# A two-layer encoder with an RWKV-7 scan: the triangular blocks inverted from blocks of 8 instead of 16

## Chip, cores and metric

The kernel runs on one core of a Trainium2 chip. The metric is the device time of one execution in microseconds (us); the kernel before was timed in three runs. Engines are named PE (TensorE, the matmul array), DVE (VectorE), ACT (ScalarE), POOL (GpSimd) and SP (SyncE, which here only issues DMAs).

## The reference, cut to what matters

Layer 0 is differential attention and a dense SwiGLU; layer 1 is two-way RWKV-7 time mixing (16 heads of 64, 272 tokens, of which 16 are learned meta tokens) and a mixture of 8 SwiGLU experts, top 2. The part at hand is the recurrence of layer 1, once forward and once backward over the tokens:

```
def _wkv7_step(S, inp):
    r, w, k, v, kk, a = inp
    sa = einsum('bhvk,bhk->bhv', S, kk)
    S = S * w - sa * (kk * a) + v * k          # outer products
    y = einsum('bhvk,bhk->bhv', S, r)
    return S, y
_, y_fwd = lax.scan(_wkv7_step, S0, (r, decay0, kd0, v, kk, a0))
_, y_bwd = lax.scan(_wkv7_step, S0, (r, decay1, kd1, v, kk, a1), reverse=True)
```

The kernel computes it by chunks of 64 tokens. Inside a chunk the steps depend on each other through a strictly triangular 64 x 64 matrix Q for each head, direction and chunk, and (1 - Q)^-1 turns the chunk's steps into a few matrix products.

## The kernel before, in words

All is float32. Layer 0 comes first, then the projections of layer 1, then the scan, then the experts, whose weights (1 MB loads by SP) are most of the data. The scan takes the 16 heads as 8 pairs (f = 0 to 7); a pair has two heads, two directions and four chunks, so 8 blocks (q) of 64 rows for each head, the first head on partitions 0 to 63, the second on 64 to 127.

A pair goes through four steps in `rwkv`:
- `rv` (L682): receptance and values by matmuls (L701), a few after each step of an earlier pair's recurrence;
- `prep` (L747): decays, rates, factors and the pairwise products, of which the masked blocks QC (L825, L833) are the Q above; `meta` (L846) makes the 16 x 16 block of the meta tokens, which goes to QD as a ninth block (L858, L859);
- `solve` (L1152): `inverse`, then `values`;
- `chain` (L965): the recurrence over the chunks, with high priority, and `norm`.
While `chain` of pair f runs, `solve` of f + 1 and `prep` of f + 2 are under way.

`inverse` (L892) works so:
- the four 16 x 16 diagonal blocks of each Q are picked out: POOL multiplies QC by a mask (L898, tile inv_p) and DVE sums over the blocks (L900, tile QD). POOL also masks QC for the first doubling level into QL (L904, one instruction for each head) and sets TD to unit matrices (L906);
- 15 rounds on DVE (L907 to L911), each a shuffle, a product and a sum that need each other in turn, solve the rows of all 9 blocks at once; round i works on 9 x (16 - i) columns, so 9 in the first and 135 in the last;
- POOL spreads TD back into 64 x 64 blocks (L913, tile T) and makes the meta tokens' Tm (L916);
- the level from 16 to 32: DVE transposes (L921), 16 matmuls with QL (L925, bank pi), ACT copies to RT (L928), 16 matmuls with RT (L932), DVE adds (L934). In the profile a float32 matmul is two records;
- the level from 32 to 64 (L937 to L963), whose result is TF, in a tile named w_raw; L963 is its last copy. `chain` begins with L990 and needs TF and Tm.

Tiles of the inverse have one buffer (QL, RT, TD, T16) or two (QC, QD, inv_b, inv_s); PSUM bank pi has one, pa two. There is one instruction stream for each engine, in order. Which order it is, the framework's planner works out ahead of the run from its own estimate of durations; the order of the calls, priorities (`CHAIN_PRIORITY`) and `issue_after` guide it. So an edit in one step can shift others within the scan.

Of the kernel before, what the change touches and what calls it, by code (L numbers as in the profile page):

```python
# [8 lines left out]
F32 = mybir.dt.float32  # L9
# [3 lines left out]
OP = mybir.AluOpType  # L13
AX = mybir.AxisListType
PSUM = bass.MemoryType.PSUM

D = 1024
NF = 8
T = 272
# [14 lines left out]
# tables that depend on the shapes alone: name -> (table, first column, columns)  # L34
LAYOUT, WIDTH = {}, [0, 0, 0, 0]
for _t, _n, _w in ((0, 'ident', 128), (1, 'ones_h', 128), (1, 'ones_d', 128), (1, 'toep', 448),
                   (2, 'bones', 128), (2, 'gmask', 384), (2, 'blk16', 64), (2, 'lev', 64), (2, 'eye16', 16),
                   (2, 'seg', 277), (2, 'sel', 128), (3, 'slot', 128), (3, 'before', 128), (3, 'one', 128), (3, 'tie', 64)):
    LAYOUT[_n] = (_t, WIDTH[_t], _w)
    WIDTH[_t] += _w  # L40


def const_tables():
    import numpy as np
    p, r = np.arange(128)[:, None], np.arange(128)[None, :]
# [10 lines left out]
    c['blk16'] = rb == cb  # L56
    c['lev'] = (rb // 2 == cb // 2) & (cb > rb)
    c['eye16'] = (p % 16) == np.arange(16)[None, :]
# [16 lines left out]
# the order of the steps that prepare a head pair's scan: of the first one, of the others  # L75
# [4 lines left out]
CHAIN_PRIORITY = 100     # how many instructions ahead of the rest of the scan the recurrence is issued  # L80


class Trunk:
# [4 lines left out]
    # ---------------------------------------------------------------- helpers  # L88
# [10 lines left out]
    def load(self, src, r0, kt, c0, nc_, pitch):  # L99
        """a [kt*128, nc_] block of a weight, as [128, kt, nc_]"""  # L100
# [4 lines left out]
    def parts(self, raw):  # L105
        """the two float32r parts of a block of up to 1024 columns"""
# [22 lines left out]
    # ---------------------------------------------------------------- LN over features on partitions  # L129
# [22 lines left out]
    def ln_end(self, pool, psum, g, b, xo, hi=None, lo=None, done=None):  # L152
        """xo(f): where the float32 result goes; hi/lo: [128, NF, T] float32r or None; done(f) follows each feature tile"""
# [42 lines left out]
    # ---------------------------------------------------------------- constants  # L196
# [31 lines left out]
    def param_rows(self, tmp):  # L228
        """per-feature parameters as they come"""
# [16 lines left out]
    def params(self, psum, tag):  # L246
        """features to the partitions"""
# [28 lines left out]
    # ---------------------------------------------------------------- layer 0  # L276
# [181 lines left out]
    def layer0(self, stack):  # L458
        """all but its last LayerNorm"""
# [66 lines left out]
        with tc.tile_pool(name="ffn", bufs=1) as fp:  # L526
# [111 lines left out]
        # first halves of the low-rank maps  # L638
# [43 lines left out]
    def rv(self, sp, psum, f, S, after=None):  # L682
        """receptance and values of head pair f, a few products after each of the given instructions"""
# [20 lines left out]
    def gates(self, sp, psum):  # L704
        """the output gate: gT holds its mixed input first"""
# [20 lines left out]
    def scan_consts(self, sp):  # L726
# [8 lines left out]
        self.QL = self.ip.tile([128, 8, 2, 64], F32, name="QL", bufs=1)  # L735
        self.RT = self.ip.tile([128, 8, 2, 64], F32, name="RT", bufs=1)
# [10 lines left out]
    def prep(self, sp, psum, f, S):  # L747
        """the factors of head pair f and their pairwise products"""
# [10 lines left out]
        QC = S['QC'] = self.ip.tile([128, 8, 64], F32, name="QC")  # L759
        QD = S['QD'] = self.ip.tile([128, 9, 16], F32, name="QD")  # L760
# [52 lines left out]
        def pairs(d):  # L813
            """pairwise products, masked: rows beta | kappa (second head kappa | beta), columns alpha | rho (rho | alpha)"""
# [3 lines left out]
            if d == 1:  # L818
                # transposed, to make it upper triangular too
# [17 lines left out]
        def turns(d):  # L837
            """beta | kappa, token-major"""
# [7 lines left out]
        def meta():  # L846
# [11 lines left out]
            nc.gpsimd.tensor_copy(QD[LO, 8, :], gsm[LO, 0, :])  # L858
            nc.gpsimd.tensor_copy(QD[HI, 8, :], gsm[HI, 1, :])  # L859
# [15 lines left out]
    def values(self, sp, psum, f, S):  # L875
        """values, token-major: chunk rows of the second head on top, of the first below"""
# [15 lines left out]
    def inverse(self, sp, psum, S):  # L892
        """(1 - Q)^-1 of the strictly upper triangular 64 x 64 blocks; those of the backward scan come out transposed"""
        nc = self.nc
        QC, QD = S['QC'], S['QD']
        b16 = self.c['blk16'].rearrange("p (b i) -> p b i", b=4)
        pr = self.ip.tile([128, 512], F32, name="inv_p", bufs=1).rearrange("p (q b i) -> p q b i", q=8, b=4)
        nc.gpsimd.tensor_tensor(pr, QC.rearrange("p q (b i) -> p q b i", b=4), b16.unsqueeze(1).to_broadcast([128, 8, 4, 16]),  # L898
                                op=OP.mult)
        nc.vector.tensor_reduce(QD[:, 0:8, :], pr.rearrange("p q b i -> p q i b"), axis=AX.X, op=OP.add)  # L900
        H = ((0, slice(0, 64)), (1, slice(64, 128)))
        QL, RT, TF = self.QL, self.RT, S['TF']
        for h, s in H:
            nc.gpsimd.tensor_tensor(QL[s, :, h, :], QC[s], self.c['lev'][s].unsqueeze(1).to_broadcast([64, 8, 64]), op=OP.mult)  # L904
        TD = self.ip.tile([128, 9, 16], F32, name="TD", bufs=1)
        nc.gpsimd.tensor_copy(TD, self.c['eye16'].unsqueeze(1).to_broadcast([128, 9, 16]))  # L906
        for i in range(15, 0, -1):  # L907
            b = self.ip.tile([128, 9, 16], F32, name="inv_b")[:, :, :16 - i]
            nc.vector.stream_shuffle(b, TD[:, :, i:16], [i] * 16 + [16 + i] * 16)
            nc.vector.tensor_tensor(b, b, QD[:, :, i:i + 1].to_broadcast([128, 9, 16 - i]), op=OP.mult)  # L910
            nc.vector.tensor_tensor(TD[:, :, i:16], TD[:, :, i:16], b, op=OP.add)  # L911
        T16 = self.ip.tile([128, 8, 64], F32, name="T16", bufs=1)
        nc.gpsimd.tensor_tensor(T16.rearrange("p q (b i) -> p q b i", b=4), TD[:, 0:8, :].unsqueeze(2).to_broadcast([128, 8, 4, 16]),  # L913
                                b16.unsqueeze(1).to_broadcast([128, 8, 4, 16]), op=OP.mult)
        Tm = S['Tm'] = sp.tile([128, 64], F32, name="Tm")
        nc.gpsimd.tensor_tensor(Tm.rearrange("p (b i) -> p b i", b=4), TD[:, 8, :].unsqueeze(1).to_broadcast([128, 4, 16]), b16,  # L916
                                op=OP.mult)
        # 16 -> 32, within masked 64 x 64 blocks
        flat = lambda t: t.rearrange("p q j -> p (q j)")
        TT = self.ip.tile([128, 512], F32, name="inv_s").rearrange("p (q j) -> p q j", q=8)  # L920
# [6 lines left out]
        for h, s in H:  # L927
            nc.scalar.copy(RT[s, :, h, :], ps[s])  # L928
# [620 lines left out]
```

## Time and profile before

| | |
|---|---|
| three runs | 1957.04, 1957.85 (median), 1960.76 us |
| profiled execution: span of its instructions | 1959.4 us; no other time is given for it |
| busy over the span | PE 1841.7 us (94%), DVE 1512.3 (77%), ACT 1186.8 (61%), POOL 632.3 (32%) |
| where the scan lies | `prep` of the first pair from about 483 us, `inverse` of the first pair from 500, last `norm` to 886 |
| experts | from about 900 us to the end |

Busy time of PE is modelled at its matmuls' ends and matmuls overlap, so a busy PE is not PE at its peak. PEclk is the clock that PE was granted as a share of 2.4 GHz; 0.5 is 1.2 GHz. "Idle before" is idle time of the engine just before an instruction, and the name after "<-" is what ended it. All times inside the trace count from the start of the span.

### The profile page before, as it was taken

The page shows a single profiled execution, that of the slowest core. Times are in us where ns is not written, and L with a number is a line of the kernel's source. Part 1 is how long each engine was busy: PE and PEld are TensorE (multiplying, and loading weights), DVE is VectorE, ACT ScalarE, POOL GpSimd, SP SyncE. Part 2 cuts the span into 40 slices and gives each one's busy share as a digit, 9 for nine tenths or more (in the row PEclk, how much of TensorE's full clock was granted, in tenths as well). Part 3 has the DMA queues.
Part 4 walks back from the last instruction along what each step waited for, and adds up shares of the span by engine and source line. Part 5 has one row for each costly group of instructions (what it writes and reads, how often), then busy time and mean ns, then how long its engine had stood idle before and what let it go on. Part 6 is the DMA issues. An engine that isn't in the chain of part 4 may idle for free. (4 is left out here: it accounts for less than half of the span.)

```text
span 1959.4 us, 30165 instructions
## 1 busy us (share of the span) xinstructions
PE 1841.7 (94%) x11332; PEld 1513.4 (77%) x11332; DVE 1512.3 (77%) x2328; ACT 1186.8 (61%) x1850; POOL 632.3 (32%) x538
## 2 busy tenths in 40 slices
PE   6999899987989989997999999999999999999996
PEld 5888899975666667776877887878878878788784
DVE  5786655587877977736888888888888888888886
ACT  4565444464254434435777777777777777777773
POOL 4322200156544634302233223232232332322323
PEclk9999899988888977898999999999999999999998
DMA  6322455521201001537899999999999999999960
GB/s 185 121 87 65 135 180 186 171 83 55 76 6 46 23 23 44 195 108 263 301 335 352 328 360 339 335 356 326 354 342 340 356 331 343 353 323 368 358 238 24
DMA packets 223997, 431.73 MB, mean 220 GB/s; under 512 B 12425, under 2 KB 77410, under 8 KB 223842
## 3 DMA queue, kind: packets, MB, share of 16 engines
q1 hardware_dynamic: 220914, 427.78, 62.5%
q10 hardware_dynamic: 2800, 1.81, 0.3%
q8 instruction: 91, 1.49, 0.3%
q0 software_dynamic: 128, 0.13, 0.1%
q14 instruction: 64, 0.52, 0.1%
HBM read 428.64 MB, written 1.05 MB: 219 GB/s over the span
## 5 line engine op out<-in xcount | busy, mean ns | idle before, releaser
L115 DVE TENSOR_TENSOR w_lo<-w_raw,w_hi 128x1024 fp32r<-128x1024 f32 (+1 forms) x632 | 884.2, 1432 | 190.4 <-ACT w_hi L112 187.1
L112 ACT CAST w_hi<-w_raw 128x1024 fp32r<-128x1024 f32 x776 | 807.0, 1049 | 332.6 <-PE pgu L124 138.4
L115 POOL TENSOR_TENSOR w_lo<-w_raw,w_hi 128x1024 fp32r<-128x1024 f32 x144 | 358.7, 2491 | 771.3 <-ACT w_hi L112 692.2
L123 PE MATMUL pgu<-w_lo,xe 128*128 128x512 f32 x896 | 356.2, 397 | 15.0 <-DVE w_lo L115 14.7
L124 PE MATMUL pgu<-w_hi,xe 128*128 128x512 f32 x896 | 353.9, 395 | 0.0
L122 PE MATMUL pgu<-w_hi,xe 128*128 128x512 f32 x896 | 349.0, 396 | 0.0
L123 PEld LDWEIGHTS pgu<-w_lo,xe 128*128 128x128 f32 x896 | 168.5, 188 | 58.1 <-DVE w_lo L115 19.0
L122 PEld LDWEIGHTS pgu<-w_hi,xe 128*128 128x128 f32 x896 | 168.4, 188 | 39.5
L124 PEld LDWEIGHTS pgu<-w_hi,xe 128*128 128x128 f32 x896 | 168.5, 188 | 39.0
L123 PE MATMUL pd<-w_lo,hth 128*128 128x512 f32 x440 | 178.1, 405 | 0.0
L124 PE MATMUL pd<-w_hi,htl 128*128 128x512 f32 x440 | 173.2, 396 | 2.3 <-DVE htl L127 2.3
L122 PE MATMUL pd<-w_hi,hth 128*128 128x512 f32 x440 | 142.1, 395 | 0.0
L124 PEld LDWEIGHTS pd<-w_hi,htl 128*128 128x128 f32 x440 | 82.2, 188 | 22.1 <-DVE htl L127 5.3
L122 PEld LDWEIGHTS pd<-w_hi,hth 128*128 128x128 f32 x440 | 82.5, 187 | 20.1
L123 PEld LDWEIGHTS pd<-w_lo,hth 128*128 128x128 f32 x440 | 82.7, 188 | 17.4
L122 PE MATMUL pj<-xh,w_hi 128*128 128x272 f32 x192 | 61.0, 318 | 8.7 <-ACT w_hi L112 5.1
L124 PE MATMUL pj<-xh,w_lo 128*128 128x272 f32 x192 | 59.1, 308 | 0.4 <-DVE w_lo L115 0.4
L123 PE MATMUL pj<-xl,w_hi 128*128 128x272 f32 x192 | 59.1, 308 | 0.0
L1330 DVE TENSOR_TENSOR hid<-hid,pgu 128x512 f32<-128x512 f32 x56 | 38.4, 686 | 20.1 <-PE pgu L124 20.0
L141 POOL COPY ln_s<-ln_y 128x272 f32<-128x272 f32 x2 | 0.8, 412 | 156.5 <-DVE ln_y L138 156.5
L701 PE MATMUL pf<-xs_v,w_raw 128*128 128x272 f32 x128 | 49.5, 518 | 0.0
L122 PEld LDWEIGHTS pj<-xh,w_hi 128*128 128x128 f32 x192 | 39.9, 208 | 10.1 <-ACT w_hi L112 5.5
(603 smaller groups left out, 3506.1 us busy)
## 6 DMA issues: line engine op xcount, KB each, us to landing
w_raw<-in_moe_w_gate_dram SPq DMA_DIRECT2D x111, 1024.0 KB, 6.7
w_raw<-in_moe_w_up_dram SPq DMA_DIRECT2D x111, 1024.0 KB, 7.3
w_raw<-in_moe_w_down_dram SPq DMA_DIRECT2D x111, 1024.0 KB, 7.0
w_raw<-in_attn_w_in_dram SPq DMA_DIRECT2D x12, 1024.0 KB, 12.2
w_raw<-in_rw_w_rkv_dram SPq DMA_DIRECT2D x12, 1024.0 KB, 5.0
w_raw<-in_ffn_w_gate_dram SPq DMA_DIRECT2D x11, 1024.0 KB, 7.9
w_raw<-in_ffn_w_up_dram SPq DMA_DIRECT2D x11, 1024.0 KB
w_raw<-in_ffn_w_down_dram SPq DMA_DIRECT2D x8, 1024.0 KB, 5.0
```

What stands on the lines that cost most here:

```text
L112: nc.scalar.copy(hi, raw)
L115: self.parted = eng.tensor_tensor(lo, raw, hi.bitcast(F32), op=OP.subtract)
L122: mm(ps, wh, xh, start=start, stop=False)
L123: mm(ps, wh, xl, start=False, stop=False)
L124: return mm(ps, wl, xh, start=False, stop=stop)
L141: nc.gpsimd.tensor_copy(self.ln_s[:, 0, :], y)
L701: nc.tensor.matmul(ps, w[:, k, o:o + 128], x[:, k, :], start=k == 0, stop=k == NF - 1)
L1330: nc.vector.tensor_tensor(s, s, ph[1], op=OP.mult)
```

## The change

The rounds stop at blocks of 8: 7 rounds instead of 15, on 9 x (8 - i) columns. A doubling level from 8 to 16 by matmuls is added in front of the level from 16 to 32; since the meta tokens' 16 x 16 block needs it too, it is now the ninth 64 x 64 block of QC (`meta` copies it there instead of to QD), and tiles of `inverse` have 9 blocks (576 columns) instead of 8 (512). QL is written twice, first with the mask of the new level, then with the old one after the first product has read it. The masked blocks pr use the two buffers of inv_s instead of inv_p. The second constants table is 56 columns wider. The rest of the diff takes comments away. Its core:

```diff
-        QC = S['QC'] = self.ip.tile([128, 8, 64], F32, name="QC")
-        QD = S['QD'] = self.ip.tile([128, 9, 16], F32, name="QD")
+        QC = S['QC'] = self.ip.tile([128, 9, 64], F32, name="QC")
+        nc.gpsimd.memset(QC[:, 8, 16:64], 0.0)
...
-            nc.gpsimd.tensor_copy(QD[LO, 8, :], gsm[LO, 0, :])
-            nc.gpsimd.tensor_copy(QD[HI, 8, :], gsm[HI, 1, :])
+            nc.gpsimd.tensor_copy(QC[LO, 8, 0:16], gsm[LO, 0, :])
+            nc.gpsimd.tensor_copy(QC[HI, 8, 0:16], gsm[HI, 1, :])
...
+        wide = lambda name, **kw: self.ip.tile([128, 576], F32, name=name, **kw).rearrange("p (q j) -> p q j", q=9)
+        pr = wide("inv_s")
+        nc.gpsimd.tensor_tensor(by8(pr), by8(QC), b8, op=OP.mult)
+        QD = self.ip.tile([128, 9, 8], F32, name="QD")
+        nc.vector.tensor_reduce(QD, by8(pr).rearrange("p q b i -> p q i b"), axis=AX.X, op=OP.add)
...
-        for i in range(15, 0, -1):
+        for h, s in H:
+            nc.gpsimd.tensor_tensor(QL[s, :, h, :], QC[s], self.c['lev8'][s].unsqueeze(1).to_broadcast([64, 9, 64]), op=OP.mult)
+        for i in range(7, 0, -1):
...
+        T8 = wide("T16", bufs=1)
+        nc.gpsimd.tensor_tensor(by8(T8), TD.unsqueeze(2).to_broadcast([128, 9, 8, 8]), b8, op=OP.mult)
+        TT = wide("inv_s")
+        nc.vector.transpose(flat(TT), flat(T8))
+        def product(left, right):
+            ps, pm = self.bank(psum).rearrange("p (q j) -> p q j", q=8), self.bank(psum, "pa")[:, 0:64]
+            for q in range(9):
+                for h, s in H:
+                    nc.tensor.matmul(ps[s, q, :] if q < 8 else pm[s], left[:, q, h, :], right[:, q, :], start=True, stop=True)
+            return ps, pm
+        ps, pm = product(QL, TT)
+        for h, s in H:
+            nc.gpsimd.tensor_tensor(QL[s, 0:8, h, :], QC[s, 0:8], self.c['lev'][s].unsqueeze(1).to_broadcast([64, 8, 64]), op=OP.mult)
+        for h, s in H:
+            nc.scalar.copy(RT[s, 0:8, h, :], ps[s])
+            nc.scalar.copy(RT[s, 8, h, :], pm[s])
+        ps, pm = product(RT, T8)
+        nc.vector.tensor_tensor(T8[:, 0:8, :], T8[:, 0:8, :], ps, op=OP.add)
         Tm = S['Tm'] = sp.tile([128, 64], F32, name="Tm")
-        nc.gpsimd.tensor_tensor(Tm ..., TD[:, 8, :] ..., b16, op=OP.mult)
+        nc.vector.tensor_tensor(Tm, T8[:, 8, :], pm, op=OP.add)
+        T16 = T8[:, 0:8, :]
```

After these lines the level from 16 to 32 goes on as before (transpose, product with QL, copy to RT, product with RT, sum).

## Rows read from the trace of the kernel before

**Rows 1.** Busy time by engine in stretches of the span: the whole scan, then four of its stretches of 10 us. Columns: stretch, length, busy time (and instructions) of PE, PE's weight loads, DVE, ACT and POOL, granted clock of PE, busy share of the DMA engines, GB/s.

```profile
495.00:895.00 400.00, 374.17 (x3643) 277.00 (x3641) 285.35 (x990) 161.30 (x502) 153.65 (x251) 0.85 0.20 71
555.00:565.00 10.00, 7.31 (x81) 6.66 (x83) 8.00 (x19) 3.03 (x8) 8.55 (x15) 0.57 0.01 2
715.00:725.00 10.00, 5.79 (x87) 4.20 (x86) 9.48 (x25) 5.13 (x14) 8.68 (x12) 0.78 0.01 2
725.00:735.00 10.00, 10.00 (x113) 6.88 (x113) 6.32 (x28) 4.68 (x16) 0.00 (x0) 0.50 0.01 3
735.00:745.00 10.00, 10.00 (x56) 6.99 (x55) 4.88 (x19) 1.79 (x6) 3.27 (x7) 0.53 0.00 1
```

**Rows 2.** The view of waits of PE, and then of DVE, in the scan (495 to 895 us): who waited for whom, us in total, times, the longest.

```profile
PE pc L1033 <- DVE R L1028: 4.7, 2, 3.3
PE pc L991 <- DVE rm L888: 4.3, 1, 4.3
PE py L1035 <- DVE R L1028: 2.5, 4, 1.3
PE py L1011 <- DVE R L986: 2.2, 5, 0.7
...
DVE R L1028 <- ACT R L1027: 17.5, 22, 2.7
DVE R L986 <- PE pc L1033: 9.9, 12, 2.2
```

**Rows 3.** The timeline of the inverse of pair 4 and of pair 7: start and length in us, engine, line, what it is. In turn: the diagonal blocks picked out, (for pair 4 only) the masking of QC by which the next pair's inverse begins, the spreading of TD after the last round, the transpose and the sum of the level from 16 to 32, and the first matmul of that pair's recurrence.

```profile
660.39 1.00 DVE L900 TENSOR_REDUCE QD<-inv_p 128x128 f32<-128x512 f32 x1
695.88 1.27 POOL L898 TENSOR_TENSOR inv_p<-QC,blob 128x512 f32<-128x512 f32 x1 [1.60 <-DVE QC L825]
705.98 1.26 POOL L913 TENSOR_TENSOR T<-TD,blob 128x512 f32<-128x512 f32 x1 [2.20 <-DVE TD L911]
708.02 0.70 DVE L921 STREAM_TRANSPOSE inv_s<-T 128x512 f32<-128x512 f32 x1
723.03 0.69 DVE L934 TENSOR_TENSOR T<-T,pi 128x512 f32<-128x512 f32 x1
741.79 0.47 PE L990 MATMUL pc<-rm,xm 64*64 64x64 f32 x2
...
800.20 1.01 DVE L900 TENSOR_REDUCE QD<-inv_p 128x128 f32<-128x512 f32 x1
824.21 1.27 POOL L913 TENSOR_TENSOR T<-TD,blob 128x512 f32<-128x512 f32 x1 [20.22 <-DVE TD L911]
825.86 0.71 DVE L921 STREAM_TRANSPOSE inv_s<-T 128x512 f32<-128x512 f32 x1
833.58 0.69 DVE L934 TENSOR_TENSOR T<-T,pi 128x512 f32<-128x512 f32 x1 [3.13 <-PE pi L932]
848.14 0.32 PE L990 MATMUL pc<-rm,xm 64*64 64x64 f32 x2
```

**Rows 4.** Groups of DVE's instructions by line and shape: the three instructions of a round, at 72 and at 135 columns (the narrowest and the widest of the eight rounds that go). Columns: times, busy us of the group, mean ns of one, idle time before.

```profile
L909 DVE STREAM_SHUFFLE inv_b<-TD 128x72 f32<-128x72 f32 x8 | 1.8, 230 | 0.1
L910 DVE TENSOR_TENSOR inv_b<-inv_b,QD 128x72 f32<-128x72 f32 x8 | 2.0, 256 | 0.3
L911 DVE TENSOR_TENSOR TD<-TD,inv_b 128x72 f32<-128x72 f32 x8 | 2.4, 304 | 0.2
L909 DVE STREAM_SHUFFLE inv_b<-TD 128x135 f32<-128x135 f32 x8 | 2.5, 314 | 0.1
L910 DVE TENSOR_TENSOR inv_b<-inv_b,QD 128x135 f32<-128x135 f32 x8 | 2.4, 304 | 0.1
L911 DVE TENSOR_TENSOR TD<-TD,inv_b 128x135 f32<-128x135 f32 x8 | 2.9, 365 | 0.1
```

**Rows 5.** The same view for DVE's other instructions of the kind that the change adds or widens: reduce, transpose, sum out of PSUM, and a 64-column operation out of PSUM.

```profile
L900 DVE TENSOR_REDUCE QD<-inv_p 128x128 f32<-128x512 f32 x8 | 8.1, 1016 | 0.0
L921 DVE STREAM_TRANSPOSE inv_s<-T 128x512 f32<-128x512 f32 x8 | 5.6, 703 | 0.6 <-POOL T L913 0.5
L934 DVE TENSOR_TENSOR T<-T,pi 128x512 f32<-128x512 f32 x8 | 5.5, 682 | 3.2 <-PE pi L932 3.1
L997 DVE COPY rm<-pc 64x64 f32<-64x64 f32 x8 | 1.8, 227 | 1.8 <-ACT rm L996 1.6
```

**Rows 6.** The timeline of PE: the first product of the level from 16 to 32 of pair 4, at full clock, and of pair 5 (the 30 records of it that follow each other), mostly at half clock.

```profile
714.95 1.15 PE L925 MATMUL pi<-inv_s,QL 128*64 128x64 f32 x32
...
759.09 1.90 PE L925 MATMUL pi<-inv_s,QL 128*64 128x64 f32 x30
```

**Rows 7.** The view by source line: instructions of ACT and POOL in the inverse, ns of one as least, median and most, first and last start, shapes.

```profile
L928 ACT COPY RT<-pi x16: 562/580/581, 534.4 to 828.6; 64x512 f32<-64x512 f32 x16
...
L898 POOL TENSOR_TENSOR inv_p<-QC,blob x8: 1266/1272/1442, 500.6 to 798.5; 128x512 f32<-128x512 f32 x8
...
L904 POOL TENSOR_TENSOR QL<-QC,blob x16: 1256/1275/1504, 501.9 to 801.2; 64x512 f32<-64x512 f32 x16
...
L916 POOL TENSOR_TENSOR Tm<-TD,blob x8: 313/322/499, 528.1 to 825.4; 128x64 f32<-128x64 f32 x8
...
L889 POOL MEMSET R<- x8: 142/145/146, 458.8 to 825.7; 64x64 f32 x8
```

**Rows 8.** The timeline of DVE and of POOL around 717 us: the same DVE instruction twice, the second beside POOL's two masks for QL.

```profile
717.23 0.42 DVE L801 SCALAR_TENSOR_TENSOR BK<-ta__7941,ep 64x256 f32<-64x256 f32 x1
717.79 1.28 DVE L801 SCALAR_TENSOR_TENSOR BK<-ta__7941,ep 64x256 f32<-64x256 f32 x1
...
717.29 2.92 POOL L904 TENSOR_TENSOR QL<-QC,blob 64x512 f32<-64x512 f32 x2
```

**Rows 9.** Busy time by engine in a stretch of the experts (columns as in rows 1), and SP's waits over the span: a weight load that waited for a product of an inverse.

```profile
1100.00:1300.00 200.00, 198.01 (x894) 160.38 (x894) 172.39 (x144) 152.16 (x164) 59.44 (x24) 1.00 0.98 346
...
SPq L102 <- PE pi L959: 23.3, 1, 23.3
```

More of the change, by code (lines that the diff above doesn't have):

```diff
@@ L36 @@
 for _t, _n, _w in ((0, 'ident', 128), (1, 'ones_h', 128), (1, 'ones_d', 128), (1, 'toep', 448),
-                   (2, 'bones', 128), (2, 'gmask', 384), (2, 'blk16', 64), (2, 'lev', 64), (2, 'eye16', 16),
+                   (2, 'bones', 128), (2, 'gmask', 384), (2, 'blk8', 64), (2, 'lev8', 64), (2, 'lev', 64), (2, 'eye8', 8),
                    (2, 'seg', 277), (2, 'sel', 128), (3, 'slot', 128), (3, 'before', 128), (3, 'one', 128), (3, 'tie', 64)):
@@ L55, in const_tables @@
     rb, cb = j // 16, r64 // 16
-    c['blk16'] = rb == cb
+    c['blk8'] = (j // 8) == (r64 // 8)
+    c['lev8'] = (rb == cb) & (r64 // 8 > j // 8)
     c['lev'] = (rb // 2 == cb // 2) & (cb > rb)
-    c['eye16'] = (p % 16) == np.arange(16)[None, :]
+    c['eye8'] = (p % 8) == np.arange(8)[None, :]
     seg = np.ones(277)
@@ L734, in scan_consts @@
         self.X = [self.kp[i // 2].tile([128, 4, 192], F32, name=f"X{i % 2}", bufs=1) for i in range(6)]
-        self.QL = self.ip.tile([128, 8, 2, 64], F32, name="QL", bufs=1)
-        self.RT = self.ip.tile([128, 8, 2, 64], F32, name="RT", bufs=1)
+        self.QL = self.ip.tile([128, 9, 2, 64], F32, name="QL", bufs=1)
+        self.RT = self.ip.tile([128, 9, 2, 64], F32, name="RT", bufs=1)
         tf = self.wraw.tile([128, 2048], F32, name="w_raw").rearrange("p (i q h j) -> p i q h j", i=2, q=8, h=2)
@@ L894, in inverse @@
         nc = self.nc
[L895 to L900, printed above, removed]
+        QC = S['QC']
@@ new lines, in inverse @@
+        wide = lambda name, **kw: self.ip.tile([128, 576], F32, name=name, **kw).rearrange("p (q j) -> p q j", q=9)
+        flat = lambda t: t.rearrange("p q j -> p (q j)")
+        by8 = lambda t: t.rearrange("p q (b i) -> p q b i", b=8)
+        b8 = self.c['blk8'].rearrange("p (b i) -> p b i", b=8).unsqueeze(1).to_broadcast([128, 9, 8, 8])
+        pr = wide("inv_s")
+        nc.gpsimd.tensor_tensor(by8(pr), by8(QC), b8, op=OP.mult)
+        QD = self.ip.tile([128, 9, 8], F32, name="QD")
+        nc.vector.tensor_reduce(QD, by8(pr).rearrange("p q b i -> p q i b"), axis=AX.X, op=OP.add)
@@ L901, in inverse @@
         H = ((0, slice(0, 64)), (1, slice(64, 128)))
         QL, RT, TF = self.QL, self.RT, S['TF']
+        TD = self.ip.tile([128, 9, 8], F32, name="TD", bufs=1)
+        nc.gpsimd.tensor_copy(TD, self.c['eye8'].unsqueeze(1).to_broadcast([128, 9, 8]))
         for h, s in H:
-            nc.gpsimd.tensor_tensor(QL[s, :, h, :], QC[s], self.c['lev'][s].unsqueeze(1).to_broadcast([64, 8, 64]), op=OP.mult)
-        TD = self.ip.tile([128, 9, 16], F32, name="TD", bufs=1)
-        nc.gpsimd.tensor_copy(TD, self.c['eye16'].unsqueeze(1).to_broadcast([128, 9, 16]))
@@ L907, in inverse @@
-        for i in range(15, 0, -1):
[L908 to L914, printed above, removed]
+            nc.gpsimd.tensor_tensor(QL[s, :, h, :], QC[s], self.c['lev8'][s].unsqueeze(1).to_broadcast([64, 9, 64]), op=OP.mult)
@@ new lines, in inverse @@
+        for i in range(7, 0, -1):
+            b = self.ip.tile([128, 9, 8], F32, name="inv_b")[:, :, :8 - i]
+            nc.vector.stream_shuffle(b, TD[:, :, i:8], [8 * k + i for k in range(4) for _ in range(8)])
+            nc.vector.tensor_tensor(b, b, QD[:, :, i:i + 1].to_broadcast([128, 9, 8 - i]), op=OP.mult)
+            nc.vector.tensor_tensor(TD[:, :, i:8], TD[:, :, i:8], b, op=OP.add)
+        T8 = wide("T16", bufs=1)
+        nc.gpsimd.tensor_tensor(by8(T8), TD.unsqueeze(2).to_broadcast([128, 9, 8, 8]), b8, op=OP.mult)
@@ L920, in inverse @@
-        TT = self.ip.tile([128, 512], F32, name="inv_s").rearrange("p (q j) -> p q j", q=8)
+        nc.vector.tensor_tensor(Tm, T8[:, 8, :], pm, op=OP.add)
+        T16 = T8[:, 0:8, :]
+        TT = wide("inv_s")[:, 0:8, :]
         nc.vector.transpose(flat(TT), flat(T16))
@@ L927, in inverse @@
         for h, s in H:
-            nc.scalar.copy(RT[s, :, h, :], ps[s])
+            nc.scalar.copy(RT[s, 0:8, h, :], ps[s])
         ps = self.bank(psum).rearrange("p (q j) -> p q j", q=8)
@@ L934, in inverse @@
         nc.vector.tensor_tensor(T16, T16, ps, op=OP.add)
-        TB = self.ip.tile([128, 512], F32, name="inv_s").rearrange("p (q j) -> p q j", q=8)
+        TB = wide("inv_s")[:, 0:8, :]
         nc.vector.transpose(flat(TB), flat(T16))
```

3 lines of the change are left out of this document (removed).

## The prediction, made before the changed kernel was run

> **What bounds the kernel now.** I read the busy time by stretches first. In the experts PE is busy 198.0 of 200 us at full clock with the DMA engines at 0.98 [rows 9]: nothing there answers to the change, and the experts' weight loads wait for tiles of the scan (SP's queue stood 23.3 us behind a product of an inverse), so a shift of the scan's end passes on one for one. The change touches only the scan, about 400 us. There PE is busy 374.2 us, idle 25.8, at a mean clock of 0.85; DVE is busy 285.4, ACT 161.3, POOL 153.7 [rows 1]. So PE bounds the scan, and two things beside its work can shrink: its idle time, and its time at half clock. A mean of 0.85 between levels of 1 and 0.5 is 30% of the scan, 120 us, at half clock. The stretches show what it follows: from 715 PE is busy 5.79 of 10 us, and in the next two stretches it is fully busy at 0.50 and 0.53 [rows 1].
>
> The waits tell who makes PE idle: four groups of PE's waits for DVE come to 4.7 + 4.3 + 2.5 + 2.2 = 13.7 us, and DVE itself waits 27.4 us in two groups for ACT and PE [rows 2]. This is a ring of the recurrence (PE, ACT, DVE, PE), whose DVE members stand in DVE's queue between rounds of a later pair's inverse. So the rounds cost PE time although no single round is what PE waits for.
>
> Last the timeline: the inverse of pair 4 takes 45.6 us from QD to T (660.39 to 705.98) and 15.7 from the level's transpose to its sum; that of pair 7 takes 23.8 (to 824.21 from the reduce's start at 800.20, call it 24.0) and 8.4 [rows 3].
>
> **What goes.** Eight of 15 rounds, those of 72 to 135 columns, three DVE instructions each. The mean of the two end widths is (230 + 314)/2 = 272 ns for the shuffle, 280 for the product, 335 for the sum [rows 4], so 0.887 us a round; 8 rounds x 8 pairs x 0.887 = 56.7 us of DVE. The seven rounds left work on the same 9 to 63 columns as the first seven before: nothing. POOL's Tm (0.32 us, [rows 7]) goes from POOL to DVE.
>
> **What comes, for each pair.** DVE: the reduce reads 576 instead of 512 columns, 1.016 x 9/8, +0.13; a transpose 0.703 x 9/8 = 0.79; a sum 0.68; Tm out of PSUM 0.23 as the nearest 64-column row [rows 5]. Together 1.83, so 14.6 for eight pairs, and DVE gets 42 us less in all.
>
> PE: two products of 18 matmuls, 72 records. 32 records took 1.15 us at full clock, 30 took 1.90 at half [rows 6]; 36 are 1.29 or 2.28, so 16 products are 20.7 to 36.5 us. At the scan's 0.85 I take 20.7/0.85 = 24. Nothing hides that: PE is the engine that is busy.
>
> ACT: two copies of 0.58 and two of 64 columns at 0.23 (taken from DVE's row, [rows 5]), 1.6, 13 in all; ACT is idle 239 us of the scan, so nothing but its place in the new level's chain. POOL: QL's first write has 9 blocks, 2 x 0.16 more; its second is 2 x 1.275 = 2.55; pr and T8 0.16 more each; the memset 0.15; Tm -0.32 [rows 7]: +3.0, 24 in all. POOL is idle 246 us of the scan, which hides it at the mean; where POOL is fully taken it costs up to these 3.0 a pair. The constants' 56 columns come with a table in layer 0 and the copies to QC replace those to QD: nothing.
>
> **New waits.** (1) QL's second write waits for PE's first product; behind it in POOL's queue stand the next pair's u, kd and BK, for which `prep` on DVE and PE waits. Bounds 0 and 2.55 a pair; I take 0, since the copy to RT, the second product, a sum and a transpose (0.58 + 1.29 + 0.68 + 0.70 = 3.3) lie before QL is read again. (2) PE's second product waits for ACT's copies; behind it stand products of the recurrence. Bounds: 0 where the planner sets other products between, 0.58 + 0.23 on two halves = 1.6 a pair; I take 0, as PE has other work nearly everywhere. (3) pr shares inv_s and so waits until the pair before has had its transpose read by L925. For pair 5 pr ran at 695.88, while L925 of pair 4 started at 714.95 [rows 3, 6]: 19 us of head start are gone as the trace stands. But the shorter rounds bring that L925 forward (below), some 12 us for pair 4, which leaves about 7, and the head start had no use while TD (one buffer) was still pair 4's until 705.98. I take 0, bound 7 on a pair like that. (4) The memset of QC waits for a buffer whose last reader, the product at L942 for two pairs before, is past by then: 0. (5) The second product's ninth block takes one of the two banks pa, which `prep` uses: 0, bound one product, 1.3. The planner lays the order anew; for that I allow 10 us either way, what one stretch of 20 us at half clock, like that from 725 to 745 [rows 1], costs or gives back.
>
> **Length of an inverse.** Eight of 15 rounds, 24 of 45 instructions: if the rest keeps its pace, the stretch from QD to T loses 45.6 x 24/45 = 24.3 us for pair 4 and 12.8 for pair 7, 18.6 in the mean. The level adds 8.4 to 15.7, mean 12, as the level from 16 to 32 takes [rows 3]. Net 6.5 shorter; the ends are 7.1 (the rounds' own time, 8 x 0.887) less 12, so 5 longer, and 18.6 less 8, so 11 shorter. The pairs overlap (chain of f beside inverse of f + 1), so this does not add up over pairs; it acts through PE's idle time and clock.
>
> **The sum.** DVE's queue loses more than half of the rounds, the wider ones. Of the 13.7 us that PE waits for DVE I let 10 go; the bounds are 0 and all 25.8 idle. The half-clock time follows idle stretches, so I let it shrink as they do, by 10/25.8, somewhat over a third: 40 us less at half clock, whose work then takes 20 at full: -20 (bounds 0 and -35). PE's new products +24. Sum -6: the profiled execution's span of 1959.4, the only time shown for it, becomes 1953.4. It lies 1.55 above the median of 1957.85, so the forecast for the median is 1952.
>
> **Rivals.** A is the forecast. **B, PE is simply the bound:** DVE's freed 42 us become idle time of DVE, the clock stays, and the 24 us on PE remain less the 10: +14, 1972. It decides as soon as PE gets back less than 24. For it: PE is busy 94% in the scan and 10.00 of 10 us from 725 to 745; the level is one more PE-ACT-PE ring for each pair. Against it: 120 us at half clock that hang on short idle stretches.
>
> **C, the level only fills PE's gaps:** the 72 records go where PE now waits (25.8 idle against 24 of new work), the recurrence keeps its times, the sum is 0: 1958. For it: totals nearly equal; against: the gaps lie in the recurrence's ring, not where the level is ready.
>
> **D, POOL's new work slows DVE:** L801 took 0.42 us by itself and 1.28 beside POOL's mask of QL, three times as long [rows 8]. In 3.0 us more of POOL a pair DVE would lose two thirds, 2.0, 16 of the 42 freed; A's 30 us of recovery shrink to 30 x 26/42 = 18.6 and the sum is +5.4: 1963. Against it: the reduce, the transpose and the ACT-bound operations need not meet the masks. The Trainium skill (SBUF — State Buffer, Who interferes with whom) says that a VectorE instruction with two SBUF inputs contends with a GpSimd instruction that reads SBUF; L801, with two such inputs, agrees by its 0.42 and 1.28. By that rule the shuffles and the transpose, with one input, would be spared, and a round's product and sum would not.
>
> **How the numbers follow.** The median can be told from no change by about 0.2%, 3.9 us. Chances: A 0.46, B 0.27, C 0.16, D 0.11. A beside the others because DVE is what the named waits end on and the clock is worth more than the idle time; B next because the new PE work is certain and its return is not. Faster: 0.41 of A, 0.02 of C, 0.01 of D = 0.44. Same: 0.05 of A, 0.02 of B, 0.12 of C, 0.04 of D = 0.23. Slower: 0.25 of B, 0.02 of C, 0.06 of D = 0.33. A's own range is 1931 (idle -16, clock -31, products at full clock +20.7: -26) to 1962. B's is 1962 to 1982 (14 and the planner's 10 each way). The range of 1931 to 1976 leaves 0.08 of A below and 0.10 of B above.
>
> **What would show it.** Right: 56 shuffles instead of 120 and DVE near 243 us in the scan; PE's matmul records up by 576; clock in the scan above 0.87; PE's waits for DVE's R and rm near 4 us; each L990 earlier than before from pair 3 on, and the last `norm` near 880 instead of 886. B shows as L990 no earlier, clock 0.85, a scan some 14 us longer with DVE idle. C: scan end unchanged, PE idle near 2. D: DVE's ns for each two-input instruction up. New waits show as PE behind RT, POOL behind the bank pi, or DVE behind inv_s. Wrong altogether if time outside 483 to 900 us changes, or if the new level takes over 20 us a pair.

## The result, and the profile after

The changed kernel took 1985.66 us (median of 4 runs, 1971.74 to 1988.24) against 1959.12 for the kernel before (4 runs): ratio 1.0123, 95% interval 1.0102 to 1.0145. It is 1.2% slower, where 1952 was forecast. The profiled execution has a span of 1984.4 us, 25.0 more than before. (The ratio is not the quotient of the two medians, which is 1.0135: one of the four runs is far shorter than the others. The two measures can differ by some tenths of a per cent.)

First the engines' totals, from the page of the changed kernel:

```profile
span 1984.4 us, 31125 instructions
PE 1864.0 (94%) x11908; PEld 1530.4 (77%) x11908; DVE 1470.6 (74%) x2096; ACT 1200.4 (60%) x1882; POOL 661.9 (33%) x554
```

Against the busy times of before (PE 1841.7, DVE 1512.3, ACT 1186.8, POOL 632.3) that is PE +22.3, DVE -41.7, ACT +13.6, POOL +29.6; the forecast had +24, -42, +13, +24. The groups that answer to [rows 5] and [rows 7] agree too (times, busy us, mean ns, idle before):

```profile
L922 DVE STREAM_TRANSPOSE inv_s<-T 128x576 f32<-128x576 f32 x8 | 6.2, 775 | 4.7 <-POOL T L919 4.6
L938 DVE TENSOR_TENSOR T<-T,pi 128x512 f32<-128x512 f32 x8 | 5.5, 688 | 12.7 <-PE pi L928 12.6
L940 DVE TENSOR_TENSOR Tm<-T,pa 128x64 f32<-128x64 f32 x8 | 1.7, 214 | 0.0
L912 POOL TENSOR_TENSOR QL<-QC,blob 64x576 f32<-64x576 f32 x16 | 22.4, 1402 | 0.6
L933 POOL TENSOR_TENSOR QL<-QC,blob 64x512 f32<-64x512 f32 x16 | 20.3, 1270 | 27.1 <-PE pi L928 22.2 <-PE pa L928 4.3
```

So the work is what it was thought to be; where it lies is not. The busy time of the scan, as in [rows 1], and of 550 to 850 us, the part in which all kernels below are in mid-scan; the second fence is the kernel before in that part:

```profile
495.00:895.00 400.00, 373.42 (x4038) 276.85 (x4037) 227.85 (x721) 167.17 (x514) 171.52 (x261) 0.85 0.17 58
550.00:850.00 300.00, 278.08 (x3169) 206.41 (x3168) 181.71 (x578) 134.55 (x418) 141.59 (x216) 0.84 0.16 55
```

```profile
550.00:850.00 300.00, 279.33 (x2906) 206.81 (x2905) 221.69 (x766) 129.07 (x409) 123.89 (x206) 0.82 0.19 65
```

DVE is relieved, but PE's idle time (26.6 of 400 us against 25.8) and its clock (0.85) are where they were. The waits of PE and of DVE in the scan (495 to 910 us), beside [rows 2]:

```profile
PE pi L969 <- DVE inv_s L960: 4.1, 2, 3.9
PE py L1034 <- DVE R L1009: 3.1, 4, 0.9
PE pa L832 <- POOL BK L804: 2.7, 2, 1.5
PE pc L1056 <- DVE R L1051: 2.5, 3, 1.3
DVE R L1051 <- ACT R L1050: 39.4, 23, 5.7
DVE R L1009 <- PE pc L1056: 18.2, 13, 2.8
```

PE's waits for DVE's R and rm did shrink, from 16.2 us (the four groups of [rows 2] and three smaller ones) to 10.0. But others came in their place, of the inverse (inv_s) and of the preparation (BK), so PE's idle time as a whole stayed. And DVE, with less to do, waits longer for the recurrence: 57.6 us in these two groups against 27.4. Now the inverses of pairs 4 and 7, beside [rows 3] (start, length in us):

```profile
650.78 0.49 ACT L769 ACTIVATE th<-pa,ptile 128x272 f32<-128x272 f32 x1 [0.93 <-PE pa L767]
678.19 0.43 DVE L827 TENSOR_TENSOR QC<-pa,blob 128x256 f32<-128x256 f32 x1 [0.19 <-PE pa L825]
681.81 1.18 DVE L905 TENSOR_REDUCE QD<-inv_s 128x72 f32<-128x576 f32 x1
693.42 1.41 POOL L919 TENSOR_TENSOR T<-TD,blob 128x576 f32<-128x576 f32 x1 [1.82 <-DVE TD L917]
695.15 0.78 DVE L922 STREAM_TRANSPOSE inv_s<-T 128x576 f32<-128x576 f32 x1
696.97 0.29 PE L928 MATMUL pa<-inv_s,QL 128*64 128x64 f32 x4
699.44 0.32 PE L928 MATMUL pa<-T,RT 128*64 128x64 f32 x4
699.67 0.69 DVE L938 TENSOR_TENSOR T<-T,pi 128x512 f32<-128x512 f32 x1 [0.90 <-PE pi L928]
699.68 0.73 PE L767 MATMUL pa<-tw,w2a 128*128 128x272 f32 x2
700.77 0.49 ACT L769 ACTIVATE th<-pa,ptile 128x272 f32<-128x272 f32 x1
729.55 0.47 PE L1013 MATMUL pc<-rm,xm 64*64 64x64 f32 x2
...
831.26 1.19 DVE L905 TENSOR_REDUCE QD<-inv_s 128x72 f32<-128x576 f32 x1
842.32 1.41 POOL L919 TENSOR_TENSOR T<-TD,blob 128x576 f32<-128x576 f32 x1 [3.69 <-DVE TD L917]
877.33 0.33 PE L1013 MATMUL pc<-rm,xm 64*64 64x64 f32 x2 [0.93 <-DVE rm L890]
```

Pair 4's stretch from QD to T is 11.6 us instead of 45.6, and its new level takes 5.2 (695.15 to the sum's end at 700.36). Yet its inverse begins 21 us later than before (681.81 against 660.39), pair 7's 31 us later. The reason is in the middle of the fence. L767 is the first matmul of the next pair's preparation; it takes a bank pa, and it follows right behind the last L928 into pa (699.44, then 699.68). So it does in every pair: the next pair's th (L769) starts at 513.5, 559.0, 601.0, 650.8, 700.8, 756.5 and 803.8 us, the sum of the new level (L938) ends at 513.4, 558.8, 600.9, 650.8, 700.4, 756.1 and 803.5. Before, nothing tied them: pair 5's th started at 669.1, 55 us ahead of pair 4's sum L934 [rows 3]:

```profile
669.14 0.49 ACT L767 ACTIVATE th<-pa,ptile 128x272 f32<-128x272 f32 x1 [0.54 <-PE pa L765]
```

Banks of one name are handed out in the order in which the program asks, and `solve` of f + 1 is written ahead of `prep` of f + 2. So preparation and inverse have become one ring: th to QC 27.4 us (650.8 to 678.2), to QD 3.6, to T 11.6, to the new sum 7.0, together 49.6 for pair 4.

The length of the scan can be taken apart into three: the first pair's first recurrence matmul (L990, L1013), the mean interval from one pair's to the next over seven intervals, and the last pair's from there to the end of its `norm`. Before: 552.6 + 7 x 42.2 + 37.8. After: 546.3 + 7 x 47.3 + 33.5. That is -6.3, +35.5, -4.3, in all +24.9 of the span's +25.0.

The mean hides where the time went. The first four intervals come to 183.3 us against 189.1 before, the last three to 147.8 against 106.3. At pair 4 the changed kernel is 12 us ahead (729.55 against 741.79), at pair 7 it is 29 behind (877.33 against 848.14). Before, the last preparations had started 33 to 57 us ahead of the previous pair's sum L934, and the last recurrences followed each other fast (39.1, 29.5 and 37.7 us apart); in the ring there is no such lead, and they stand 51.5, 49.7 and 46.6 apart.

The table gives head, interval, tail and the clock from 550 to 850 us for all runs. These four are of one profiled execution of each kernel, which can lie some us from the median of its runs (x1's 9 above, x11's 9 below, y3's 5 below, those of y4, z1 and z2 5 to 7 above). A ratio is to runs of the kernel before that were taken beside it:

```
run (edit)                          median   ratio [95%]               head   interval  tail  clock
before                              1959.1                             552.6  42.2      37.8  0.82
after                               1985.7   1.0123 [1.0102, 1.0145]   546.3  47.3      33.5  0.84
x1  after, ninth block in py        1966.9   1.0040 [1.0014, 1.0066]   545.3  45.4      37.7  0.89
x2  before, two uses of pa          2016.0   1.0275 [1.0241, 1.0309]   548.4  51.9      31.2  0.78
x3  before, level's products twice  1991.3   1.0153 [1.0128, 1.0178]   554.8  45.5      41.9  0.82
x4  before, 7 rounds                1932.6   0.9870 [0.9851, 0.9889]   527.0  41.7      37.9  0.89
x5  after, no ninth block           1957.1   1.0006 [0.9983, 1.0028]   537.6  44.1      32.4  0.93
x6  after, ninth block in pf        1968.0   1.0052 [1.0035, 1.0070]   555.7  42.8      37.8  0.88
x7  x6, pr in a buffer of its own   1979.3   1.0134 [1.0094, 1.0173]   553.5  44.8      37.9  0.88
x8  before, matmuls added to rv     1964.9   1.0045 [1.0030, 1.0059]   558.5  41.7      37.8  0.87
x9  before, 7 rounds in pair 0      1963.1   1.0039 [1.0017, 1.0061]   529.3  45.0      41.9  0.85
x10 before, 7 rounds in the others  1961.2   1.0024 [1.0001, 1.0047]   552.4  42.0      37.8  0.82
x11 new inverse in pair 0 alone     1973.6   1.0088 [1.0063, 1.0113]   540.9  44.3      37.8  0.86
x12 before, priority 80             1964.7   1.0029 [1.0003, 1.0056]   550.9  43.2      36.4  0.81
y1  after, meta block at the end    1966.9   1.0047 [1.0029, 1.0066]   550.5  44.1      34.9  0.90
y2  before, one product twice       1989.1   1.0133 [1.0101, 1.0166]   550.5  46.0      41.9  0.77
y3  after, priority 120             1953.9   0.9967 [0.9951, 0.9982]   539.8  42.8      32.4  0.92
y4  x5, priority 120                1962.7   1.0000 [0.9974, 1.0027]   541.6  45.4      34.6  0.88
z1  before, priority 120            1957.6   0.9994 [0.9976, 1.0012]   553.1  43.1      34.6  0.82
z2  after, priority 140             1956.9   0.9990 [0.9970, 1.0011]   547.0  43.1      36.0  0.93
```

### The profile page after: what moved, and what is told of

Read it like the earlier page. It is cut to its first block, busy times and chain, and to the rows that moved or that the text cites. A ratio compares the mean times of both kernels' runs of the same rounds, so it can differ in the third digit from the quotient of the medians.

```text
span 1984.4 us, 31125 instructions
## 1 busy us (share of the span) xinstructions
PE 1864.0 (94%) x11908; PEld 1530.4 (77%) x11908; DVE 1470.6 (74%) x2096; ACT 1200.4 (60%) x1882; POOL 661.9 (33%) x554
## 5 line engine op out<-in xcount | busy, mean ns | idle before, releaser
L124 PE MATMUL pgu<-w_lo,xe 128*128 128x512 f32 x896 | 356.0, 397 | 13.9 <-DVE w_lo L116 13.6
L832 PE MATMUL pa<-X,BK 128*128 128x128 f32 x256 | 46.0, 342 | 2.8 <-POOL BK L804 2.7
L832 PEld LDWEIGHTS pa<-X,BK 128*128 128x128 f32 x256 | 41.5, 246 | 6.8 <-POOL BK L804 3.8
```

What stands on the lines that cost most here:

```text
L124: mm(ps, wh, xl, start=False, stop=False)
L832: S['paired'] = nc.tensor.matmul(pg[:, c, :], BK[:, c, h, :], X[:, c, 64 * h:64 * h + 128], start=True, stop=True)
```

## The experiments

**Is it the bank?** x1:

```diff
-            ps, pm = ..., self.bank(psum, "pa")[:, 0:64]
+            ps, pm = ..., next(pms)     # the unused half of the pair's bank py
```

> The changed kernel, but the ninth blocks of the two new products go to the unused half of the bank py of the pair's own parity instead of to the banks pa. Theory R (ring): in the changed kernel the first matmul of the preparation of pair f + 2 takes the bank pa that the ninth block of pair f + 1 leaves, so preparation and inverse alternate with a fixed period of about 49 us per pair; without it the preparation runs ahead again, the last chain ends near 880 us instead of 904 and the time falls from 1985 to 1950 to 1962. Rival B (PE's 24 us of new products are the bound): the time stays within 5 us of the changed kernel's, 1980 to 1990. Rival P (the masked blocks pr wait in inv_s): also no change.

It took 1966.9, 7 above before, 19 below after; th starts 6 to 17 us ahead of the new sum again. The expectation of 1950 to 1962 was missed by 5: in pair 2 the ninth matmuls waited until 613.1 us for the `norm` of pair 0 to have read py, so this place has a wait of its own.

x2, the same dependence put into the kernel before, with hardly any work:

```diff
+        pms = [self.bank(psum, "pa")[:, 0:64] for _ in range(2)]
+        sc = self.ip.tile([128, 64], F32, name="sc")
+        for pm in pms:
+            for h, s in H:
+                nc.tensor.matmul(pm[s], QL[:, 0, h, :], TT[:, 0, :], start=True, stop=True)
+            nc.scalar.copy(sc, pm)
```

> The kernel before, with two small products (two matmuls of 64 x 64 each) into the banks pa set behind the first product of the level from 16 to 32 in each inverse, and a copy of each by ACT; nothing reads the copies. 32 matmul records and 16 copies more in all, some 5 us of engine time. Theory R: the preparation of pair f + 2 again has to wait for the inverse of pair f + 1, and the time rises by 15 to 40 us, to 1975 to 2000. Rival B: not over 5 us more, 1958 to 1964.

It took 57 us more, beyond the range expected (its 32 matmuls are 64 records, not 32). Its timeline where pair 2's inverse meets pair 3's preparation:

```profile
634.60 0.40 PE L931 MATMUL pa<-inv_s,QL 128*64 128x64 f32 x8
636.02 0.46 ACT L932 COPY sc<-pa 128x64 f32<-128x64 f32 x2
637.17 0.72 PE L765 MATMUL pa<-tw,w2a 128*128 128x272 f32 x2
638.00 0.49 ACT L767 ACTIVATE th<-pa,ptile 128x272 f32<-128x272 f32 x1 [1.52 <-PE pa L765]
```

L765, the preparation's first matmul, starts 0.7 us after the second copy has read its bank (636.48, then 637.17), and th at 638.0 instead of 584.4 in the kernel before. The interval is 51.9 us, and recurrences that used to overlap (pair 1's began 26 us before pair 0's was done) now stand 14 us or more apart. With 15 rounds in the ring it is longer than the changed kernel's. It was run at this one priority, so what part of the 57 us hangs on the order is open.

x5 leaves out the ninth block's products, and so every use of pa (Tm's upper right block is left out with them):

> The changed kernel without the ninth block's part of the two new products: 8 of 72 records a pair go, and with them every use of the banks pa by the inverse; Tm is a copy of its 8 x 8 blocks (its upper right block is left out). Theory R (the bank pa): the preparation runs ahead again and the time falls from 1985 to 1950 to 1965, at or a little below that of the kernel with the ninth block in py (1967), whose ninth block waited for the norm of two pairs before. Theory B alone (PE's new work is the bound): 1980 to 1984, as 8 records are 0.3 us a pair.

1.0006, as expected: the loss is gone, but there is no gain. Its timeline has pair 4's th 25 us ahead of pair 3's new sum:

```profile
624.82 0.49 ACT L769 ACTIVATE th<-pa,ptile 128x272 f32<-128x272 f32 x1 [0.39 <-PE pa L767]
...
649.73 0.69 DVE L937 TENSOR_TENSOR T<-T,pi 128x512 f32<-128x512 f32 x1 [2.39 <-PE pi L928]
```

x6 (`pm` from bank pf) and y1 (the ninth block through pi, behind the level from 32 to 64; inv_b gets one buffer) keep the whole computation without pa:

> The changed kernel with the ninth blocks in bank pf, which the receptance and value matmuls use, instead of in pa. Theory R: preparation does not wait; the receptance and value matmuls, which are wanted late, wait instead. 1950 to 1967. If any shared bank costs what pa costs, 1980 to 1990.

> The changed kernel, with the ninth block's part of the two new products done at the end of the inverse through the bank pi (8 records a pair, two copies and a sum moved there), so that the inverse does not use pa at all. Nothing is left out. If the bank pa is what costs 25 us, 1950 to 1966, as in the run without the ninth block (1957); if the ninth block's work itself costs, 1970 or more.

1968.0 and 1966.9: some 18 us of the 26 come back, a little past the upper end of both expectations. Each has a new cost of its own: in x6 the interval is near that of before (42.8), but the head is 9 us longer than the changed kernel's; in y1 POOL's first mask into QL waits 22.7 us in five times for the ninth block, now at the end of the inverse, to have read QL. x7 gave pr its own buffer beside x6 (`pr = wide("inv_p", bufs=1)`), and to make room three other tiles (QD, inv_b, gn_s) one buffer instead of two:

> As the kernel with the ninth blocks in pf, and the masked blocks pr have a buffer of their own again (three other small tiles get one buffer instead of two to make room). If pr's wait for the pair before costs time, 5 to 15 us below the kernel with pf alone; by the forecast, which took 0 for this wait, the same within 4 us.

11 us slower than x6 instead of faster or equal, and 22 slower than the kernel before, without the ring. Its trace shows one wait that x6 has hardly: POOL stands 29.6 us in four times, once 19.2, in front of the memset of a later pair's QC, until PE's L969 has read the old one (x6: 2.8 us in two). Whether that is the price is not shown, since buffers and order changed together. So x7 does not price pr's wait; it made the order a suspect.

**Is it PE's new work?** x3 and y2 issue the level's products of the kernel before twice (`for q in [*range(8)] * 2`), both of them or the first alone; x8 adds three matmuls of 272 columns a pair to `rv`, a similar PE time, but away from the inverse:

```diff
+                    for j in range(0 if k else 1 + i):
+                        nc.tensor.matmul(ps, w[:, k, o:o + 128], x[:, k, :], start=True, stop=True)
```

> The kernel before, with the two products of the level from 16 to 32 issued twice each into the same bank: 64 matmul records more for each pair, some 2.3 us of PE for a pair at full clock, 21 in all, and no other work or wait. Rival B: the time rises by 18 to 30 us, to 1977 to 1989. Theory R says nothing of PE's price; if R is the whole cause, the rise is small, 0 to 10 us (1958 to 1968).

> The kernel before, with three more matmuls of 272 columns in front of each pair's receptance and values, whose results are overwritten: 6 records of 0.36 us for each pair, 2.2 us of PE as in the kernel with the doubled level products, but away from the inverse and with nobody waiting for it. If PE's time as such is the bound (B), the time rises by 16 to 24 us, to 1975 to 1983. If the doubled products cost 32 us because they stand in the chain of the inverse, it rises by less than 10 us.

> The kernel before with only the first product of the level from 16 to 32 issued twice: 32 records more a pair, half of the run with both doubled (+32 us). If the price goes with the records in the inverse, +12 to +20 (1970 to 1978); if the +32 was mostly an unlucky order, anything from 0 to 10 (1956 to 1968).

+32 for 64 records a pair, +29 for 32 (both above every range expected), and +7 for x8, whose 48 records are busy 16.4 us in its trace. So PE's time as such is not the bound that rival B made of it, as x5 and (below) y3 also say, which carry 64 and 72 new records a pair without the loss; and in the inverse the price does not go with the records. x8 seems to have got part back through the clock (0.87 against 0.82; by my estimate 0.05 of 300 us are 15 us at full clock), y2 to have lost by it (0.77). What remains of x3 and y2 beyond their records is not settled.

**Are DVE's rounds worth what the forecast gave them?** x4 leaves eight rounds out everywhere (`range(15, 8, -1)`), x9 in the first pair alone, x10 in the others alone:

> The kernel before, with only the first seven of the 15 rounds (the wider eight are left out, and with them rows of the inverse): 57 us of DVE and the length of the inverse go, nothing comes. If DVE's rounds are worth time in the scan, as the forecast had it, the time falls by 20 to 40 us, to 1918 to 1938; if another order or PE bounds the scan, by less than 10.

> The kernel before, with seven of 15 rounds in the inverse of the first pair alone (the wider eight are left out there, 7 us of DVE). Theory S (start): what the shorter rounds gave in the run with seven rounds in all pairs (27 us) is the head of the scan, where the first pair's inverse runs with no recurrence beside it: its first recurrence began 25.6 us earlier, and the interval from pair to pair stayed at 42. Then this run gains 12 to 25 us: 1933 to 1946. Theory D (my forecast: DVE's rounds hold up PE in all pairs): an eighth of 27 us, 1952 to 1958.

> The kernel before, with seven of 15 rounds in the inverses of the other seven pairs (the wider eight are left out there, 50 us of DVE). Theory S: 0 to 8 us faster, 1950 to 1960. Theory D: 20 to 27 us faster, 1931 to 1939.

All: -27, near the forecast's -30 for idle time and clock, and with the clock at 0.89; but by the table 25.6 us of it lie in the head. And one part and the other each give nothing (+5, +3), so both theories fail. The table says how: x9's first recurrence starts 23 us earlier and loses it in the intervals (45.0) and the tail; x10 has the old head and the old interval. Only together does the early head meet intervals that can keep it. x11, the new inverse for the first pair alone, went as x9 (head -11.7, interval 44.3, in the fastest of its four runs) and took 15 us more than before where 5 to 18 less were expected:

> The first pair inverted as in the changed kernel (7 rounds and the level from 8 to 16) but its meta block by 15 rounds of its own behind it, with no use of pa; the other pairs as before. Theory S: the head of the scan is 7 to 18 us shorter and the rest unchanged, 1940 to 1953, faster than both kernels. Theory D: no change beyond 4 us.

**Is it the order?** The recurrence's priority, `CHAIN_PRIORITY`, sets how far the planner issues it ahead; nothing else changes.

> The kernel before with one number of the planner changed: the recurrence's priority is 80 instructions instead of 100. The same instructions in another order; it measures what a new order alone does. My estimate in the forecast was 10 us either way (1949 to 1969); if the differences of up to 15 us between the kernels above hang on the order, this run moves by over 5 us.

> The changed kernel with the recurrence's priority at 120 instructions instead of 100: another order of the same instructions. If the bank pa sets its pace, it stays within 8 us of 1985 (1977 to 1993); if its time was an unlucky order, it may fall to 1960 to 1970.

> The run without the ninth block's products (1957), with the priority at 120: 1950 to 1966 if the order moves a kernel by up to 8 us, as it moved the kernel before by 5.7; and at least 15 us below the changed kernel with the same priority.

> The kernel before with the recurrence's priority at 120. Its order differs from that at 100 in far fewer places than that at 80 did. If the order alone moves a kernel by some 6 us, 1952 to 1966; if 120 is better for any kernel, 1935 to 1950, and the change then is slower at both priorities.

> The changed kernel with the priority at 140. If a recurrence that goes further ahead leaves the preparation short and steady (interval 41.4 from pair to pair in the run at 120), 1946 to 1960; if 120 was one lucky order, anywhere up to 1985.

The kernel before moves by some 6 us (1964.7 at 80, 1957.6 at 120). The changed kernel falls by 32, to 1953.9 at 120, below both ranges expected, and by 29, to 1956.9, at 140. At 120 it is a little faster than the kernel before at 100 (0.9967); against that at 120 (z1, 0.9994) its lead is at the edge of the noise. It is the one version here that computes all and lies below the kernel before by more than the noise. So my theory that the bank as such sets the pace fell with y3, and so did the second half of y4's expectation. It is not that the ring was gone; pair 3's level and pair 4's preparation in y3:

```profile
640.18 0.29 PE L928 MATMUL pa<-T,RT 128*64 128x64 f32 x4
640.39 0.73 PE L767 MATMUL pa<-tw,w2a 128*128 128x272 f32 x2
641.00 0.21 DVE L940 TENSOR_TENSOR Tm<-T,pa 128x64 f32<-128x64 f32 x1
641.22 0.49 ACT L769 ACTIVATE th<-pa,ptile 128x272 f32<-128x272 f32 x1 [2.14 <-PE pa L767]
649.72 1.16 PE L832 MATMUL pa<-X,BK 128*128 128x128 f32 x8
651.76 1.05 PE L832 MATMUL pa<-X,BK 128*128 128x128 f32 x8
656.87 0.41 DVE L827 TENSOR_TENSOR QC<-pa,blob 128x256 f32<-128x256 f32 x1
```

The bank is handed on just so, but th to QC takes 15.7 us instead of 27.4, and the whole ring 41.4; four intervals running are of 41.4 to 41.7 us. The same products L832 at priority 100, with two waits of PE and POOL's factor BK ahead of them:

```profile
660.50 0.57 PE L1058 MATMUL py<-R,GA 128*64 128x64 f32 x4 [1.27 <-DVE R L1051]
662.55 1.61 POOL L804 TENSOR_TENSOR BK<-kd,ep 64x256 f32<-64x256 f32 x2
663.07 0.70 PE L1056 MATMUL pc<-R,TK 128*64 128x64 f32 x8 [1.04 <-DVE R L1051]
665.93 3.78 PE L832 MATMUL pa<-X,BK 128*128 128x128 f32 x16
```

The next two fences are the busy time by engine in those stretches, of the changed kernel and of y3 (columns as in [rows 1]):

```profile
655.00:665.00 10.00, 7.14 (x106) 4.94 (x105) 8.75 (x19) 6.36 (x18) 9.38 (x17) 0.90 0.15 53
665.00:675.00 10.00, 10.00 (x87) 8.10 (x86) 3.47 (x11) 2.73 (x9) 1.91 (x5) 0.67 0.00 0
675.00:685.00 10.00, 8.88 (x87) 6.60 (x85) 6.99 (x18) 2.75 (x11) 5.12 (x8) 0.92 0.31 107
```

```profile
641.00:651.00 10.00, 9.89 (x133) 7.37 (x134) 8.63 (x22) 8.28 (x23) 7.76 (x14) 1.00 0.33 107
651.00:661.00 10.00, 10.00 (x158) 7.67 (x157) 6.98 (x19) 3.74 (x15) 8.55 (x15) 1.00 0.01 2
550.00:850.00 300.00, 285.42 (x3472) 214.83 (x3471) 186.60 (x604) 141.94 (x445) 140.99 (x217) 0.92 0.19 66
```

At priority 100 PE stands for 2.9 us, 2.3 of them for R of the recurrence, and then works at a clock of 0.67: L832's 16 records at 665.93 take 3.78 us, the same products in y3 2.2. At 120 PE is hardly idle and stays at full clock. By my estimate the difference of 0.08 in the clock is, over 300 us, 24 us of PE at full speed, most of the 32.

But the clock is not all of it. More than half of the 11.7 us lies ahead of the slow products: th to the first L832 takes 15.1 us at 100 and 8.5 at 120. In the order at 100 POOL, which is busy 9.38 of the 10 us, makes other factors first and starts on BK, which L832 needs, 11.8 us after th (662.55), in y3 7.8 (648.99). It is so in pairs 3 to 6: th to L832 takes 12.2 to 15.1 us in the changed kernel, 8.5 to 9.8 in y3 and z2, and th to the new sum 47.0 to 55.4 us against 39.7 to 42.9.

A slow preparation alone costs little: x5 has the same at 100 (11.8 to 15.0 us from th to L832 in pairs 1 to 7, 44 to 70 to the sum), but there pairs overlap and the interval is 44.1. And where the order keeps the ring short, the bank costs nothing: y4, without the ring, is no faster than y3.

## Why the prediction was wrong

The failed step is **wait (5)**: the ninth block takes one of the two banks pa, "0, bound one product, 1.3". I priced how long the bank is held. Its cost is the order that it makes: a preparation that started 19 to 57 us ahead of the previous pair's sum L934 now starts behind the sum of the new level. The same dependence, put into the kernel before, cost 57 us (x2, shown), and without it the changed kernel is level with before (x5, shown) or within 11 us of it (x1, x6, y1). Every one of these edits also made the planner lay a new order, and x7 lost 22 us without the ring; so the ring is one way to lose here, not the only one.

With it fails the **allowance for a new order**, 10 us either way. It holds for the kernel before (x12, z1), but a closed ring takes on whatever the order does to it: 32 us between priorities 100 and 120. So the loss has two conditions, the ring and an order in which the preparation inside it is slow (POOL's factor late, PE waiting and then below full clock); y3 and z2 have the first without the second, x5 the second without the first, and none of them has the loss.

Taken by steps at priority 100, the runs give the forecast's sum so: the shorter rounds alone -27 (x4), the new level without the ninth block +24.5 on top of that (x5 against x4), and from there to the changed kernel +28.6. The first two stood in the sum at -30 and +24; the third is the term that stood at 0. As each step also changes the order, none of the three is sure to better than some 6 us.

The others, one by one. **Engine terms** were right, within 6 us each (first fence). **The length of an inverse** was right in sign and too cautious: over the eight pairs QD to T fell from 35.0 to 12.1 us in the mean, 22.9 where 18.6 were said (pair 4 lost 34.0 for 24.3, pair 7 13.0 for 12.8), and the new level took 7.4 where 12 were. Pair 7's 23.8 in the prediction is the 24.0 named beside it. **The recoveries**, 10 of idle time and 20 of clock, did not come: idle 26.6, clock 0.85. Part of the mechanism is there: PE's waits for R and rm fell by 6 us, y3 got the clock to 0.92, and 1953.9 is near the 1952 forecast. But that agreement is luck, of y3's order: x4's 27 us lie in the head, and x9 and x10 show that the rounds' gain is not spread over the pairs as I had it. **PE's +24** as a plain addend was wrong in both directions: 7 for x8, 32 for x3. **Rival B** had the right sign and 1972, and two of its signs came, the clock at 0.85 and DVE's freed time idle; but the changed kernel lies 14 above it, and its mechanism is not borne out (x8, x5, y3). **C** (1958) missed: PE's idle time is 26.6 us, not near 2. **D**: [rows 8] do not show L801 by itself: its first 0.42 us there ran beside POOL's mask too, from 717.29 on. The 0.42 holds all the same, as two of them took 0.84 us at 726.48, while POOL did nothing [rows 1]. L803 answers to L801; its 32 instructions take 21.0 us in sum against 19.1, so the contention grew by 2 us there, a small part of the 16 that D took. **Waits (1) to (4)**: (1) POOL did wait 26.5 us for the first product (L933 in the group above), but no wait of PE for QL shows above 1 us. (2) No wait of PE for the new level's RT shows. (3) POOL's idle time in front of pr ends on DVE's QC and rm (7.7 and 3.8 us), never on a reader of inv_s, so 0 holds as far as the trace shows; x7 does not settle its price. (4) The memset of QC was not always free: POOL stood 2.8 us in front of it here, 16.2 in x5, 29.6 in x7.

Open as well: why the planner's order at 100 puts BK late, which of BK, PE's waits and the clock weighs how much inside the ring, and the share of order in x2, x3, x7 and y2.

## What to carry to other kernels

When an edit lets one stage take a buffer or bank from a rotation that another stage uses, ask which stage asks first in program order and how far the other one used to run ahead: that lead is what can be lost, not the time that the bank is held. Whether it is lost depends on how short the resulting ring can be kept. Where a planner orders the instructions, run both versions at two or three priorities before a difference of 1% is put down to the edit. And take the span apart into head, interval and tail: a shorter head is worth nothing when the intervals cannot keep it.

## What the runs showed that was not expected

PE work put away from the inverse may pay for part of itself: with x8's 16.4 us the clock in mid-scan is 0.87 instead of 0.82, and the cost is 7.4; one run, with an order of its own, does not prove it. And some of these kernels scatter more than others: x1's ten runs lie between 1954.83 and 1976.40 us, y4's ten between 1944.76 and 1968.52, those of the kernel before, 13 beside x1, between 1956.92 and 1962.36. Why is open.
